# A hybrid DeltaNet and attention layer on one core: sixteen TensorE instructions placed behind named projection matmuls

## Chip, cores and metric

The kernel runs on one core of one Trainium2 chip. The metric is the device time of the whole program in microseconds (us). The kernel before takes 1417.83 us, the median of three runs (1417.33 to 1420.5).

## What is computed

One decoder layer over 1024 tokens of width 1024, all in fp32. Cut to what matters here:

```
u   = rms_norm(h) @ W_in                # one projection, columns shared out to both groups
oA  = gated delta rule                  # 4 heads of 128: conv, decay, chunks of 64, a state
        value, k_cumdecay = solve(eye + lower, rhs)      # unit lower triangular
        step: v_new = value_i - kcd_i @ state
              o     = q_i @ state + intra_i @ v_new
              state = state * exp(gl_i) + k_i^T @ v_new
oB  = diff attention                    # 4 heads, two causal softmax maps of 64 per head
        a = softmax(q1 k1) - lam * softmax(q2 k2);  out = a @ v
h   = h + concat(oA, oB) @ W_out
h   = h + W_down(silu(g) * v),  [g, v] = causal_dwconv3(rms_norm(h) @ W_up)
```

## The kernel before

Tokens are worked on in eight tiles of 128 (`NT`). A number in fp32 is split into a high and a low part, and a product is three TensorE matmuls: high times high, low times high, high times low. So a projection is a long row of matmuls that depend on nothing but loaded weights and the normalised input. Two kinds fill the first half of the program: `gT` (128x512, lines L434 to L436, a head's columns with the tokens along the row) and `pn` (128x256, L415, L416 and L418, tokens along the partitions). In the second half `pwo` (128x512, L395 to L397) multiplies by W_out, and `pe` (L1248 to L1250, in `up_early`) is the first of the products of the up projection.

Stages by time in the profiled execution: first norm up to 45 us; first projections to 95 us; the delta rule of four heads to 385 us; differential attention of four heads from 395 to 675 us; W_out, the second norm and its transposes (`tr`, L257, in `wout_b`) to 745 us; then `up` in 22 blocks and `down` to the end.

The latency-bound parts of a stage are chains through several engines, and projection matmuls lie between their steps on TensorE. In the delta rule, `delta_prep` transposes keys and values (`pk` L625, `pv` L671), `delta_inverse` solves the triangular systems (`pz` L744, L759 and others, each step through VectorE), `delta_scan` steps through the chunks (`pP` L772, `pzz` L776, `pS`, `po` L793; ScalarE evacuates `s` at L781 and the outputs at L794), and `delta_out` scales the output by the gate `szh` (loaded L807, ScalarE L808, GpSimd L809, VectorE L813) and transposes it (`omT` L819). In attention, `qk_norm` and `qk_stack` scale, rotate and stack queries and keys (VectorE L861 to L877, L887, GpSimd L864, ScalarE L886 and L888) and transpose them (`pT` L896, copied out by ScalarE as `K` and `Q` at L897); `attn1` makes a tile of scores (`S` L921, L922, a mask L924), its row maxima (VectorE L926 or L928) and its exponentials `p` (ScalarE L931); `attn2` transposes `p` (`paT` L949) and multiplies by the values (`pao` L954). PSUM gives the scores in attention two tiles, so a third tile of scores can start only when the exponentials of the first are made. `wout_b` adds `pwo` to the residual row (VectorE L1141), scales it (`u` L287) and transposes it (`tr` L257).

Nobody writes the order of the queues by hand: a scheduler takes the instructions one by one by priority (the table `PRI`, applied by `part(name)`) and by its own estimate of when their inputs are there, and puts each on its engine's queue. Each engine works through its queue in order: an instruction that waits holds all that stands behind it on that engine. What of the filler stands ahead of a waiting instruction is therefore fixed when the program is built. All matmuls and transposes go to TensorE directly (`PE = nc.tensor`); `psG`, `psS` and `sm` hand out the PSUM tiles of the stages up to the second norm, `bank` those after it.

Of the kernel before, what the change touches and what calls it, by code (L numbers as in the profile page):

```python
# [10 lines left out]
F32 = mybir.dt.float32  # L11
# [7 lines left out]
P = 128  # L19
# [22 lines left out]
PP0, PP1 = 4, 2  # L42
PRE_K = {5: 1, 6: 0}

A_AT = [(1, 0), (1, 2), (1, 4), (1, 5), (2, 4), (2, 6), (3, 0), (3, 2), (3, 3)]


# [17 lines left out]
def hybrid_layer(ctx, tc, x, positions, norm1_w, w_in, dn_conv_w, dn_a_log, dn_dt_bias,  # L65
                 dn_norm_w, df_q_norm_w, df_k_norm_w, df_lambda_q1, df_lambda_k1,
                 df_lambda_q2, df_lambda_k2, df_subln_w, w_out, norm2_w, w_up, ffn_conv_w,
                 ffn_conv_b, w_down, cst, out, dbg=None, stop=None):
    nc = tc.nc
    V, S, G, PE = nc.vector, nc.scalar, nc.gpsimd, nc.tensor  # L70
    DMA = nc.sync
    dbg = dbg or {}

# [11 lines left out]
    pq = pctx.enter_context(tc.tile_pool(name="pq", bufs=2, space=bass.MemoryType.PSUM))  # L85

    sctx = ExitStack()
    pS = [sctx.enter_context(tc.tile_pool(name="pS", bufs=2, space=bass.MemoryType.PSUM)), 512]
    @contextmanager
    def part(name):  # L90
        p = tc.cur_priority
        q = max(0, p - PRI[name])
        tc.cur_priority = q
        yield
        tc.cur_priority = p + tc.cur_priority - q
# [3 lines left out]
    def nm(s):  # L99
        uid[0] += 1  # L100
        return f"{s}_{uid[0]}"

    def gt(s, shape=(P, T), dt=F32):
        return gp.tile(list(shape), dt, tag="g", name=nm(s))

    def gtr(s):
        return gt(s, dt=F32R)
# [4 lines left out]
    def ct_(s, dt=F32):  # L112
        return cq.tile([P, T], dt, tag="c", name=nm(s))

    def lt(s):
        return lp.tile([P, T], F32, tag="l", name=nm(s))
# [8 lines left out]
        return wp.tile([P, T], F32R, tag="w", name=nm(s))  # L125

    def psG(s="pG"):
        return pq.tile([P, 512], F32, tag="G", name=nm(s), bufs=2)

    def psS(s="pS"):  # L130
        return pS[0].tile([P, pS[1]], F32, tag="S", name=nm(s), bufs=2048 // pS[1])

    def sm(s="sm"):
        return pq.tile([P, 512], F32, tag="t", name=nm(s), bufs=2)

    def small(s, w, bufs=2, dt=F32):
        return sp.tile([P, w], dt, tag=s, name=nm(s), bufs=bufs)
# [69 lines left out]
    def split_w(raw, lo_eng=None, w=T, alloc=None):  # L207
        hi, lo = ((alloc or wt)(s)[:, 0:w] for s in ("whi", "wlo"))
        S.activation(hi, raw[:, 0:w], AF.Copy)  # L209
        if lo_eng is DMA:  # L210

            S.activation(lo, raw[:, 0:w], AF.Copy, scale=-1.0)
            G.dma_start(lo.bitcast(F32), raw[:, 0:w], accum_op=ALU.add)
        elif lo_eng is G:
            G.tensor_tensor(lo, raw[:, 0:w], hi.bitcast(F32), op=ALU.subtract)  # L215
        else:
            V.tensor_tensor(lo, raw[:, 0:w], hi.bitcast(F32), op=ALU.subtract)  # L217
        return hi, lo
# [84 lines left out]
    for k0 in range(0, NK, 3):  # L303
        n = min(3, NK - k0)
# [10 lines left out]
    with tc.manual_schedule(engines={mybir.EngineType.Activation}):  # L315
        for tt in range(NT + 1):
# [7 lines left out]
            if 0 < tt < 4:  # L324
                k = tt - 1
                n = min(3, NK - 3 * k)
# [67 lines left out]
    def mm3(ps, lh, ll, rh, rl, first, last):  # L394
        PE.matmul(ps, lh, rh, start=first, stop=False)  # L395
        PE.matmul(ps, lh, rl, start=False, stop=False)  # L396
        PE.matmul(ps, ll, rh, start=False, stop=last)  # L397
# [43 lines left out]
    def proj_T(h, kind):  # L441
        ct = kind * 4 + h
        st = praw[ct] = ct_("pT")
        for q, o in gemm_T(win, ct * P, xn, lambda q: psG("gT"), DMA):
            S.activation(st[:, q * 512:(q + 1) * 512], o, AF.Copy)
            yield

    def steps(gen, n=99):
        for _ in range(n):
            if next(gen, gen) is gen:  # L450
                break
# [589 lines left out]
    def mix_mm(hl, wf):  # L1041
        ps = psG("pwo")
        for k in range(4):
            wh, wl = wf(k)
            mm3(ps, hl[:, k * P:(k + 1) * P], hl[:, 512 + k * P:512 + (k + 1) * P], wh, wl, k == 0, k == 3)
        return ps
# [104 lines left out]
    def attention():  # L1151
# [27 lines left out]
        for h in range(4):  # L1179
            pr = prep(h + 1) if h < 3 else None  # L1180
            for n, tt in enumerate(range(NT) if h < 3 else reversed(range(NT))):
# [5 lines left out]
                if pr is not None and (PP1 <= n < PP1 + 4 if h > 0 else n >= PP0):  # L1187
                    with part("prep"):
                        steps(pr, 1)
                if (h, n) in A_AT:  # L1190
                    with part("wa"):
# [24 lines left out]
    if stop == "norm2":  # L1216
# [3 lines left out]
    pf = [ctx.enter_context(tc.tile_pool(name=f"pf{i}", bufs=4, space=bass.MemoryType.PSUM, reuse_waits="tile"))  # L1220
          for i in range(2)]

    def bank(i, s):
        return pf[i % 2].tile([P, 512], F32, tag="b", name=nm(s))


    act_dram = dp.tile([FFN, T], F32, name="act_dram")
# [28 lines left out]
    def raw_(s="raw"):  # L1256
        return rp.tile([P, T], F32, tag="raw", name=nm(s))
# [79 lines left out]
    def down():  # L1337
        pairs = [(i, i + 1) for i in range(0, NF, 2)]
        kept = None
        for c in range(2):  # L1340
            cs = slice(c * 512, (c + 1) * 512)
            pss = [bank(tt // 4, "pd") for tt in range(NT)]
            order = pairs if c == 0 else pairs[::-1]
            for pr in order:
                raw = raw_()
                nc.sync.dma_start(raw.rearrange("p (k c) -> p k c", c=512),
                                  wdn[pr[0] * P:(pr[0] + 2) * P, cs].rearrange("(k p) c -> p k c", p=P))
                wh, wl = (t.rearrange("p (k c) -> p k c", c=512) for t in split_w(raw))
                if kept is not None:
                    hl, kept = kept, None  # L1350
                else:
                    hl = []
                    for i in pr:
                        g_ = raw_("act") if c == 0 and pr is order[0] else ct_("act")
                        nc.sync.dma_start(g_, act_dram[i * P:(i + 1) * P, :])
                        gh, gl = gtr("gh"), gtr("gl")
                        S.activation(gh, g_, AF.Copy)  # L1357
                        V.tensor_tensor(gl, g_, gh.bitcast(F32), op=ALU.subtract)  # L1358
                        hl.append((gh, gl))

                def mm(tt, i):
                    ts_ = slice(tt * P, tt * P + P)
                    gh, gl = hl[i]
                    mm3(pss[tt], gh[:, ts_], gl[:, ts_], wh[:, i], wl[:, i],
                        pr is order[0] and i == 0, pr is order[-1] and i == 1)


                tis = [(tt, i) for i in range(2) for tt in range(NT)]
                for tt, i in sorted(tis) if pr is order[-1] else tis:
                    mm(tt, i)  # L1370
            if c == 0:
                kept = hl
            for q in range(4):
                res = lt("fres") if q < 2 else gt("fres")
                rv = res.rearrange("p (t c) -> p t c", c=512)
                rows = slice(q * 256, (q + 1) * 256)
                nc.sync.dma_start(rv, h_dram[rows, cs].rearrange("(t p) c -> p t c", p=P))
                for i in range(2):
                    tt = q * 2 + i
                    V.tensor_tensor(rv[:, i, :], pss[tt], rv[:, i, :], op=ALU.add)  # L1380
                    nc.sync.dma_start(out2[tt * P:(tt + 1) * P, cs], rv[:, i, :])
# [6 lines left out]
    for j in range(NF):  # L1388
        up(j, early[j] if j < EARLY else None)
    down()  # L1390


# [26 lines left out]
```

## Time and profile before

| | |
|---|---|
| median of three runs | 1417.83 us (1417.33 to 1420.5) |
| the profiled execution, its own time | 1418.1 us |
| its span (first to last instruction) | 1416.3 us |
| TensorE (PE) busy | 1337.9 us, 94% |
| VectorE (DVE) busy | 830.9 us, 59% |
| ScalarE (ACT) busy | 634.8 us, 45% |
| GpSimd (POOL) busy | 335.7 us, 24% |
| mean granted TensorE clock | 0.980 of full |

Busy shares are averages over stages that differ. A row of the timeline shows an instruction's start, its duration, its engine and line, what it writes and reads, and in brackets how long its engine stood idle just before it and what ended that. PE is TensorE's matmuls, PEld its weight loads.

### The profile page before, as it was taken

How to read it: one execution, taken by the hardware profiler on the slowest of the kernel's cores; microseconds unless marked ns; L12 is line 12 of the kernel's file. 1: busy time of each engine (PE TensorE's matmuls, PEld its weight loads, DVE VectorE, ACT ScalarE, POOL GpSimd, SP SyncE). 2: the span in 40 equal slices, each digit the busy share in tenths (PEclk: the TensorE clock that was granted, in tenths of full speed). 3: DMA queues.
4: the chain of work that ended last, by engine and by line, in shares of the span. 5: the costliest groups of instructions: out<-in, count | busy, mean ns of one | idle time of the engine just before them, and what ended most of it. 6: DMA issues, size and time to landing. Idle time of an engine off the chain costs nothing. (4 is left out here: it accounts for less than half of the span.)

```text
span 1416.3 us, 21566 instructions
## 1 busy us (share of the span) xinstructions
PE 1337.9 (94%) x8439; PEld 1127.0 (80%) x8439; DVE 830.9 (59%) x1630; ACT 634.8 (45%) x1142; POOL 335.7 (24%) x271
## 2 busy tenths in 40 slices
PE   7999999989979998999878899999999989999998
PEld 7877777878979986778656788888888878888887
DVE  6427767854443368877787666666666666334331
ACT  6467565532234455664544444444444444222220
POOL 3021101120341254240032434444333430000000
PEclk8999999999989999999988999999999999999999
DMA  7353233221733358444421222222222247557421
GB/s 228 89 122 80 64 84 75 76 76 60 210 98 94 106 142 217 113 132 149 142 90 43 80 86 76 89 82 82 89 75 85 79 140 268 172 157 229 137 86 60
DMA packets 145269, 161.54 MB, mean 114 GB/s; under 512 B 9487, under 2 KB 114703, under 8 KB 145167
## 3 DMA queue, kind: packets, MB, share of 16 engines
q1 hardware_dynamic: 130959, 144.21, 32.0%
q0 software_dynamic: 12736, 14.68, 5.6%
q8 instruction: 66, 1.08, 0.3%
q10 hardware_dynamic: 1472, 1.27, 0.3%
q14 instruction: 36, 0.29, 0.1%
HBM read 111.36 MB, written 38.29 MB: 106 GB/s over the span
## 5 line engine op out<-in xcount | busy, mean ns | idle before, releaser
L395 PE MATMUL pd<-whi,gh 128*128 128x512 f32 x352 | 136.9, 389 | 0.0
L396 PE MATMUL pd<-wlo,gh 128*128 128x512 f32 x352 | 136.9, 389 | 0.0
L397 PE MATMUL pd<-whi,gl 128*128 128x512 f32 x352 | 136.9, 389 | 0.0
L415 PE MATMUL pn<-whi,xn 128*128 128x256 f32 x448 | 115.8, 292 | 0.2 <-ACT whi L209 0.2
L416 PE MATMUL pn<-whi,xn 128*128 128x256 f32 x448 | 114.7, 290 | 0.0
L1334 POOL TENSOR_TENSOR acc<-acc,acc 128x1024 f32<-128x1024 f32 x22 | 53.6, 2437 | 242.1 <-issue 215.5
L1357 ACT ACTIVATE gh<-act 128x1024 fp32r<-128x1024 f32 x42 | 44.4, 1060 | 123.9 <-PE pd L396 104.3
L1358 DVE TENSOR_TENSOR gl<-act,gh 128x1024 fp32r<-128x1024 f32 x42 | 52.0, 1241 | 68.0 <-ACT gh L1357 67.7
L415 PEld LDWEIGHTS pn<-whi,xn 128*128 128x128 f32 x448 | 86.9, 195 | 0.7 <-ACT whi L209 0.4
L416 PEld LDWEIGHTS pn<-whi,xn 128*128 128x128 f32 x448 | 86.6, 194 | 0.3
L209 ACT ACTIVATE whi<-raw 128x1024 fp32r<-128x1024 f32 x58 | 61.0, 1053 | 53.1 <-PE pn L416 19.3
L215 POOL TENSOR_TENSOR wlo<-raw,whi 128x1024 fp32r<-128x1024 f32 x22 | 53.2, 2432 | 115.1 <-issue 46.2
L209 ACT ACTIVATE whi<-rx 128x1024 fp32r<-128x1024 f32 x22 | 23.3, 1061 | 127.1 <-POOL rx L1289 127.1
L1248 PE MATMUL pa<-xT,whi 128*128 128x512 f32 x176 | 70.0, 398 | 9.3 <-ACT xT L1121 5.3
L434 PE MATMUL gT<-xn,whi 128*128 128x512 f32 x192 | 77.9, 406 | 0.0
L435 PE MATMUL gT<-xn,whi 128*128 128x512 f32 x192 | 77.6, 404 | 0.0
L436 PE MATMUL gT<-xn,wlo 128*128 128x512 f32 x192 | 77.2, 402 | 0.2 <-DMA wlo<-raw 0.2
L217 DVE TENSOR_TENSOR wlo<-rx,whi 128x1024 fp32r<-128x1024 f32 x22 | 28.9, 1315 | 82.2 <-ACT whi L209 82.1
L395 PEld LDWEIGHTS pd<-whi,gh 128*128 128x128 f32 x352 | 66.1, 188 | 13.8
L396 PEld LDWEIGHTS pd<-wlo,gh 128*128 128x128 f32 x352 | 66.1, 188 | 13.8
L397 PEld LDWEIGHTS pd<-whi,gl 128*128 128x128 f32 x352 | 66.1, 188 | 13.5
L418 PE MATMUL pn<-wlo,xn 128*128 128x256 f32 x448 | 72.4, 296 | 1.5 <-POOL wlo L215 1.5
(380 smaller groups left out, 3691.7 us busy)
## 6 DMA issues: line engine op xcount, KB each, us to landing
act<-act_dram SPq DMA_DIRECT2D x42, 512.0 KB, 4.6
rw<-in_w_up_dram SPq DMA_DIRECT2D x22, 512.0 KB, 3.8
act_dram<-acc SPq DMA_DIRECT2D x22, 512.0 KB, 2.6
raw<-in_w_down_dram SPq DMA_DIRECT2D x22, 512.0 KB, 4.4
raw<-in_w_in_dram SPq DMA_DIRECT2D x18, 512.0 KB, 3.9
pn_dram<-pn SPq DMA_DIRECT2D x16, 512.0 KB, 3.4
wlo<-raw POOLq DMA_DIRECT2D x12, 512.0 KB, 4.6
rx<-in_w_up_dram SPq DMA_DIRECT2D x22, 256.0 KB, 3.0
```

The lines of the kernel that those rows point to most:

```text
L209: S.activation(hi, raw[:, 0:w], AF.Copy)
L395: PE.matmul(ps, lh, rh, start=first, stop=False)
L396: PE.matmul(ps, lh, rl, start=False, stop=False)
L397: PE.matmul(ps, ll, rh, start=False, stop=last)
L415: PE.matmul(o, xs(xn, 0, kt, a, b), wh, start=kt == 0, stop=False)
L416: PE.matmul(o, xs(xn, 1, kt, a, b), wh, start=False, stop=False)
L418: PE.matmul(o, xs(xn, 0, kt, a, b), wf(kt)[1], start=False, stop=kt == NK - 1)
L434: PE.matmul(o, whi[:, kt, :], xs(x_, 0, kt, *qs), start=kt == 0, stop=False)
L435: PE.matmul(o, whi[:, kt, :], xs(x_, 1, kt, *qs), start=False, stop=False)
L436: PE.matmul(o, wlo[:, kt, :], xs(x_, 0, kt, *qs), start=False, stop=kt == NK - 1)
L1248: PE.matmul(ps, wh[:, ks], xh[k], start=first, stop=False, skip_group_check=not start)
L1334: G.tensor_tensor(accs[1], accs[0], accs[1], op=ALU.mult)
```

## The change

A table `BEHIND` names sixteen TensorE instructions, each by a kind of PSUM tile, which tile of that kind, and which instruction into it; and for each another instruction behind which it must stand on the queue. To count them, `PE` becomes a small class that hands each matmul or transpose on to `nc.tensor` and notes it under the tile that it writes. At the end `order_banks()` gives the scheduler sixteen extra order edges without a semaphore. Nothing is computed otherwise, and each engine issues the same instructions as before: 7396 on PE, 1604 on DVE, 972 on ACT.

```diff
+BEHIND = [
+    ("pk", 0, 0, "gT", 9, 12), ("pv", 0, 0, "gT", 11, 3), ("pz", 0, 0, "gT", 14, 22), ("pz2", 1, 0, "gT", 21, 1),
+    ("pzz", 16, 0, "pn", 10, 25), ("omT", 4, 0, "pn", 13, 30), ("S", 0, 1, "pn", 23, 11), ("S", 1, 1, "pn", 23, 11), ("pT", 4, 0, "pn", 24, 47),
+    ("S", 17, 0, "pwo", 3, 11), ("pT", 20, 0, "pwo", 7, 2), ("S", 30, 0, "pwo", 9, 11), ("tr", 18, 0, "pwo", 24, 4),
+    ("tr", 20, 0, "pwo", 26, 9), ("tr", 22, 0, "pwo", 28, 9), ("tr", 29, 0, "pe", 0, 23),
+]
...
-    V, S, G, PE = nc.vector, nc.scalar, nc.gpsimd, nc.tensor
+    V, S, G = nc.vector, nc.scalar, nc.gpsimd
+    banks, by_bank = {}, {}
+    class PE:
+        @staticmethod
+        def note(out, ins):
+            by_bank.setdefault(out.tensor.name.rsplit("_", 1)[0], []).append(ins.ins)
+        @staticmethod
+        def matmul(out, *a, **k):
+            PE.note(out, nc.tensor.matmul(out, *a, **k))
...
+    def bank_name(s):
+        banks.setdefault(s, []).append(nm(s))
+        return banks[s][-1]
+    def order_banks():
+        at = lambda s, n, k: by_bank[banks[s][n]][k]
+        for *x, s, n, k in BEHIND:
+            tc.add_manual_dep(at(*x), at(s, n, k).name,
+                              mybir.DependencyInfo(mybir.DependencyClass.NoSync, mybir.DependencyReason.DATA),
+                              reason="order")
...
-        return pq.tile([P, 512], F32, tag="t", name=nm(s), bufs=2)
+        return pq.tile([P, 512], F32, tag="t", name=bank_name(s), bufs=2)
...
     for j in range(NF):
         up(j, early[j] if j < EARLY else None)
     down()
+    order_banks()
```

(The same edit of the name stands in `psG`, `psS` and `bank`.) The changed file is longer at its head, so a line of the kernel before has a number 36 higher in the change, and all matmuls there carry line L90, all transposes L94, those of the class `PE`.

Since the scheduler takes the other engines' instructions by when their inputs come, their queues change too. Three places follow.

The first is the end of the scan of the third head, on PE. `omT_509` are the transposes of that head's gated output, `pn_593` and `pn_594` two tiles of the next head's projection, `pv1_517` a step of the fourth head's triangular solve. Before:

```order
L415 MATMUL pn_593_3946<-whi_590_3941,xn_14_138 128x256
L732 MATMUL pv1_517_3679<-inv1_511_3504,U_438_3277 32x32 x16
L416 MATMUL pn_593_3946<-whi_590_3941,xn_15_139 128x256
L418 MATMUL pn_593_3946<-wlo_588_3935,xn_14_138 128x256
L819 MATMUL omT_509_3488<-k_sb_96,acc_292_2245 128x128
L418 MATMUL pn_593_3946<-wlo_588_3935,xn_14_138 128x256
```

Now:

```order
L90 MATMUL pn_594_3996<-whi_587_3934,xn_14_138 128x256
L90 MATMUL pn_594_3996<-whi_587_3934,xn_15_139 128x256
L90 MATMUL pn_594_3996<-whi_587_3934,xn_14_138 128x256
L94 MATMUL omT_509_3488<-k_sb_96,acc_292_2245 128x128 x4
L94 MATMUL omT_510_3495<-k_sb_96,acc_292_2245 128x128 x4
L90 MATMUL pv1_517_3679<-inv1_511_3504,U_438_3277 32x32 x16
```

Seven matmuls of `pn_593` and 31 of `pn_594` have come to stand ahead of the transposes, and the sixteen of `pv1_517` behind them.

The second is the same place on ACT, where `s128` and `acc<-po` are the two steps of the scan's last chunks (L781 and L794 before), `szh_508` and `szh_583` the gates of the third and fourth head, and `pn_418` the projection whose columns they are loaded from. Before:

```order
L421 ACTIVATE pn_418_3086<-pn_420_3137 128x512
L209 ACTIVATE whi_599_4151<-raw_598_4149 128x1024
L781 ACTIVATE s128_503_3454<-pzz_502_3452,cj_304_2308 128x128
L794 ACTIVATE acc_292_2245<-po_504_3456,sqs_306_2313 128x128
L713 ACTIVATE inv1_511_3504<-pv0_513_3537 128x256
L800 ACTIVATE dec_271_2044<-acc_292_2245 128x1024
L713 ACTIVATE inv1_511_3504<-pv0_515_3607 128x256
L808 ACTIVATE szh_508_3476<-szh_508_3476 128x1024
L736 ACTIVATE U_438_3277<-inv1_511_3504 32x8x32 x4
L808 ACTIVATE szh_583_3899<-szh_583_3899 128x1024
```

Now:

```order
L457 ACTIVATE pn_418_3086<-pn_420_3137 128x512
L245 ACTIVATE whi_599_4151<-raw_598_4149 128x1024
L817 ACTIVATE s128_479_3400<-pzz_478_3398,cj_304_2308 128x128
...
L830 ACTIVATE acc_292_2245<-po_499_3444,sqs_306_2313 128x128
L844 ACTIVATE szh_508_3476<-szh_508_3476 128x1024
L817 ACTIVATE s128_503_3454<-pzz_502_3452,cj_304_2308 128x128
L844 ACTIVATE szh_583_3899<-szh_583_3899 128x1024
L830 ACTIVATE acc_292_2245<-po_504_3456,sqs_306_2313 128x128
```

The two gates now stand ahead of the last two steps of the scan, and the copy of `pn_418` three chunks earlier than it did.

The third is the start of attention, on PE. `pT_635` to `pT_638` are the transposes of the first head's second half of keys and queries, `S_664` its third tile of scores (`S_643` and `S_657` are the first two), `pn_673` and `pn_684` projections of the values. Before:

```order
L415 MATMUL pn_673_4777<-whi_670_4772,xn_14_138 128x256
L416 MATMUL pn_673_4777<-whi_670_4772,xn_15_139 128x256
L896 MATMUL pT_635_4465<-k_sb_96,stk_634_4460 128x128 x4
L896 MATMUL pT_636_4473<-k_sb_96,stk_634_4460 128x128 x4
...
L418 MATMUL pn_673_4777<-wlo_671_4773,xn_14_138 128x256
L896 MATMUL pT_637_4481<-k_sb_96,stq_633_4459 128x128 x4
L896 MATMUL pT_638_4487<-k_sb_96,stq_633_4459 128x128 x4
L921 MATMUL S_664_4698<-K_610_4365,Q_614_4369 128x384
```

Now:

```order
L90 MATMUL pn_673_4777<-whi_667_4765,xn_15_139 128x256
L90 MATMUL S_664_4698<-K_610_4365,Q_614_4369 128x384
L90 MATMUL S_664_4698<-K_612_4367,Q_614_4369 128x384
...
L90 MATMUL S_683_4841<-K_610_4365,Q_614_4369 128x512
...
L90 MATMUL pn_673_4777<-wlo_671_4773,xn_14_138 128x256 x4
L94 MATMUL pT_635_4465<-k_sb_96,stk_634_4460 128x128 x4
L94 MATMUL pT_636_4473<-k_sb_96,stk_634_4460 128x128 x4
L90 MATMUL pn_684_4854<-whi_667_4765,xn_14_138 128x256
```

`S_664` and the fourth tile `S_683`, which stood behind the transposes, now stand ahead of them and ahead of 36 matmuls of `pn_673`. On DVE, at the same place, the multiplication L861 of the queries and keys, which stood behind the row maxima of `S_643` and `S_657`, now stands ahead of them.

## Rows read from the trace of the kernel before

**Rows 1.** The page's first part: busy time of TensorE over the span.

```profile
PE 1337.9 (94%) x8439; PEld 1127.0 (80%) x8439; DVE 830.9 (59%) x1630; ACT 634.8 (45%) x1142; POOL 335.7 (24%) x271
```

**Rows 2.** Windows: length; PE, PEld, DVE, ACT, POOL busy; granted clock; DMA share, GB/s.

```profile
312.00:330.00 18.00, 13.13 (x156) 11.47 (x157) 9.68 (x18) 5.34 (x9) 5.42 (x4) 0.81 0.25 86
400.00:426.00 26.00, 18.64 (x122) 17.81 (x121) 12.35 (x23) 7.59 (x16) 10.63 (x9) 0.80 0.40 92
534.00:544.00 10.00, 7.64 (x35) 6.22 (x36) 9.56 (x21) 6.70 (x16) 3.89 (x5) 0.83 0.86 235
726.00:738.00 12.00, 7.69 (x25) 5.92 (x25) 9.01 (x17) 9.00 (x15) 4.60 (x4) 0.72 0.35 110
440.00:480.00 40.00, 39.86 (x321) 38.67 (x320) 15.15 (x30) 15.42 (x30) 13.54 (x7) 1.00 0.25 73
850.00:900.00 50.00, 50.00 (x221) 41.13 (x220) 30.69 (x33) 20.79 (x23) 21.79 (x15) 1.00 0.26 84
```

**Rows 3.** Timeline of PE, the delta rule: three of five waiting instructions.

```profile
104.72 0.77 PE L625 MATMUL pk<-k_sb,acc 128*128 128x128 f32 x5 [1.67 <-ACT acc L589]
121.40 0.77 PE L671 MATMUL pv<-k_sb,acc 128*128 128x128 f32 x5 [0.95 <-ACT acc L589]
...
282.74 0.49 PE L776 MATMUL pzz<-nv,U 128*128 128x128 f32 x2 [0.92 <-DVE U L761]
```

**Rows 4.** Timeline of PE, the third head's output transposes.

```profile
317.18 0.33 PE L819 MATMUL omT<-k_sb,acc 128*128 128x128 f32 x1 [2.88 <-DVE acc L813]
320.06 0.47 PE L819 MATMUL omT<-k_sb,acc 128*128 128x128 f32 x1 [1.98 <-DVE acc L813]
```

**Rows 5.** Timeline of ACT around the end of that scan.

```profile
295.60 0.37 ACT L781 ACTIVATE s<-pzz,cj 128x128 f32<-128x128 f32 x1 [1.60 <-DVE s L780]
...
302.47 0.59 ACT L421 ACTIVATE pn<-pn 128x512 f32<-128x512 f32 x1
303.89 0.37 ACT L781 ACTIVATE s<-pzz,cj 128x128 f32<-128x128 f32 x1
313.17 1.06 ACT L808 ACTIVATE szh<-szh 128x1024 f32<-128x1024 f32 x1 [3.35 <-DMA szh<-pn_dram]
```

**Rows 6.** Timeline of PE, the start of attention.

```profile
403.61 0.30 PE L922 MATMUL S<-K,Q 128*128 128x128 f32 x1 [2.82 <-DMA K<-K]
419.62 1.11 PE L896 MATMUL pT<-k_sb,stk 128*128 128x128 f32 x4 [4.54 <-DVE stk L887]
```

**Rows 7.** Timeline of DVE, same stretch.

```profile
406.33 0.42 DVE L928 TENSOR_REDUCE nmx<-S 128x2 f32<-128x256 f32 x1 [3.92 <-PE S L924]
```

**Rows 8.** Timeline of ACT, same stretch.

```profile
418.21 0.63 ACT L886 ACTIVATE stk<-qk 128x512 fp32r<-128x512 f32 x1 [4.43 <-DVE qk L877]
...
421.03 1.19 ACT L897 ACTIVATE K<-pT 128x512 fp32r<-128x512 f32 x2
422.12 0.36 ACT L931 ACTIVATE p<-S,nmx 128x128 f32<-128x128 f32 x1
```

**Rows 9.** Timeline of PE, attention of the second and third head.

```profile
536.36 0.50 PE L921 MATMUL S<-K,Q 128*128 128x512 f32 x1 [3.97 <-ACT p L931]
558.59 0.87 PE L896 MATMUL pT<-k_sb,stk 128*128 128x128 f32 x6 [2.36 <-DVE stk L887]
590.00 0.50 PE L921 MATMUL S<-K,Q 128*128 128x512 f32 x1 [1.32 <-ACT p L931]
```

**Rows 10.** Timeline of PE, transposes of the second norm.

```profile
685.46 0.73 PE L257 MATMUL tr<-k_sb,u 128*128 128x128 f32 x5 [0.95 <-DVE u L287]
...
705.45 0.98 PE L257 MATMUL tr<-k_sb,u 128*128 128x128 f32 x7 [2.30 <-DVE u L287]
730.44 0.87 PE L257 MATMUL tr<-k_sb,u 128*128 128x128 f32 x3 [4.31 <-DVE x L1119]
743.64 1.08 PE L257 MATMUL tr<-k_sb,u 128*128 128x128 f32 x4 [4.57 <-DVE u L287]
```

**Rows 11.** PE's waits between 95 and 750 us: us, times, longest.

```profile
PE pwo L395 <- ACT mhl L1072: 0.7, 1, 0.7
```

More of the change, by code (lines that the diff above doesn't have):

```diff
@@ L69, in hybrid_layer, with transpose @@
     nc = tc.nc
-    V, S, G, PE = nc.vector, nc.scalar, nc.gpsimd, nc.tensor
+    V, S, G = nc.vector, nc.scalar, nc.gpsimd
[7 more added lines that the diff above has]
+            PE.note(out, nc.tensor.matmul(out, *a, **k))
+        @staticmethod
+        def transpose(out, *a, **k):
+            PE.note(out, nc.tensor.transpose(out, *a, **k))
+    def bank_name(s):
[7 more added lines that the diff above has]
+                              reason="order")
     DMA = nc.sync
@@ L127, in psG @@
     def psG(s="pG"):
-        return pq.tile([P, 512], F32, tag="G", name=nm(s), bufs=2)
+        return pq.tile([P, 512], F32, tag="G", name=bank_name(s), bufs=2)
     def psS(s="pS"):
-        return pS[0].tile([P, pS[1]], F32, tag="S", name=nm(s), bufs=2048 // pS[1])
+        return pS[0].tile([P, pS[1]], F32, tag="S", name=bank_name(s), bufs=2048 // pS[1])
     def sm(s="sm"):
-        return pq.tile([P, 512], F32, tag="t", name=nm(s), bufs=2)
+        return pq.tile([P, 512], F32, tag="t", name=bank_name(s), bufs=2)
     def small(s, w, bufs=2, dt=F32):
@@ L1223, in bank @@
     def bank(i, s):
-        return pf[i % 2].tile([P, 512], F32, tag="b", name=nm(s))
+        return pf[i % 2].tile([P, 512], F32, tag="b", name=bank_name(s))
     act_dram = dp.tile([FFN, T], F32, name="act_dram")
```

## The prediction

> **What bounds the kernel.** I read the page's busy table first: TensorE is busy 1337.9 of 1416.3 us [rows 1], so no order of its queue can take off more than the 78.4 us in which it stands idle, and what runs at half clock. [...] Then the timeline of PE, stall by stall: in each row of [rows 3, 4, 6, 9] the bracket says that PE stood before an instruction whose input another engine made late. From the order I then read how much filler now stands ahead of each.
>
> The sum is made against the profiled execution's own time, 1418.1 us, 0.3 above the median. A measurement of this kernel can tell about 0.2% (2.8 us) from no change.
>
> **What the change does to the sum.** It adds no instruction. It moves filler from behind a waiting instruction to ahead of it. That work is borrowed: it would have run later anyway, and where the two orders meet again (before attention, and at the first block of `up`) nothing is left of it. The time gained is idle time truly filled; it is lost again where the next release comes no earlier than before, since PE then waits there instead. If every release stayed at its old time, the gain at any point could be no more than the filler borrowed up to it. If releases move forward with PE, each stall is a gain of its own. That gives two ends for each place.
>
> *Delta rule, first five* [rows 3]: five stalls from 1.67 to 0.92 us, of which three are shown and two between them are like the last, together 5.7. `pk` and `pv` each have eight `gT` more ahead of them, 8 x 0.226 = 1.8 us. It is the same debt carried on, so with fixed releases both together gain 1.8 and not 2.6, and before the fourth stall, where four `gT` (0.9 us) are left of it, only 0.9. Ends: 1.8 (0.9 kept and 0.9 at `pzz`, with 27 `pn` ahead) and 5.7. I take **3.0**, nearer the low end, because the releasers, ACT and DVE, run chains of their own here.
>
> *Output of the third head* [rows 4]: 2.88 + 1.98 = 4.86 us of stall. 38 `pn` now stand ahead, 38 x 0.124 = 4.7 us. The release comes earlier too: the gate `szh` came in at 313.17 us, 10.7 us after `pn` was copied at 302.47 [rows 5], and that copy now stands ahead of the step of the scan that ran at 295.60, three chunks earlier, at about 294. So both stalls go. A new wait takes part of it: the two gates now stand on ACT ahead of the last steps of the scan (303.89 us before). The landing comes to about 294 + 10.7 = 304.7, then two gates of 1.06 us pass first; behind them wait the scan's last `po` on PE and the `pv0` behind it. I price that at 2.0 us (from 0 to 4.9). The window of 312 to 330 us has a clock of 0.81, so 0.19 x 18 = 3.4 us may be had back; I take half, 1.7. Together **4.6**, ends 0 and 8.3.
>
> *Start of attention* [rows 6]: 2.82 + 4.54 = 7.4 us of stall. Ahead of the first score tile stand 24 `pn` more (3.0 us), ahead of `pT` 36 (4.5 us): both covered. But two score tiles come ahead of `pT`, and they need the exponentials of the first two. PE stood before `pT` at 419.62 - 4.54 = 415.1; it will stand before `S_664` four `pn` (0.5 us) and the filled 2.8 us earlier, at 411.8. The exponential it needs ended at 422.12 + 0.36 = 422.5 [rows 8]. Two things bring that forward. The 1.19 us copy of `K` stood ahead of it on ACT and no longer does. And DVE waited 3.92 us for the first scores [rows 7] with the key and query work queued behind; that work now goes first, so the chain through GpSimd to `stk` comes up to 3.9 us earlier. That makes 417.4, a new stall of 5.6 us in place of 7.4. With some 0.8 us for a weight split that moved behind a copy on ACT, I take **1.0**, and nothing of the clock (0.80 in that window), since a stall of 5.6 remains. Ends: 422.5 - 411.8 = 10.7, a loss of 3.3; and 7.4 plus 0.20 x 26 = 5.2 of clock, 12.6.
>
> *Attention, three stalls* [rows 9]: 3.97 + 2.36 + 1.32 = 7.7 us, with 14, 19 and 21 `pwo` more ahead (3.2, 4.3, 4.7 us; the first has eight `pT` besides). They are covered. But in the window around the first DVE is busy 9.56 of 10 us, and so it is, nearly, around the third [rows 2]: there PE waits for an engine that is full. What is filled there leaves less filler for the score and value products that follow. I take half of the stalls, 3.8, and half of the clock's 0.17 x 10 = 1.7 at the first and as much at the third, 3.4 in all: together **5.5**; ends 0 and 11.1. [...]
>
> *Second norm* [rows 10]: the first three `tr` waited 0.95, 2.30 and 2.30, 5.6 us in all (the second, like the third, is not shown). They get 5, 10 and 10 `pwo` ahead (1.1, 2.3, 2.3 us), covered all but exactly. Those `pwo` wait for their own split; one such wait shows in the trace, 0.7 us [rows 11]. Three of them leave **3.4**; ends 0 and 5.6.
>
> *Last pin* [rows 10]: twelve `pe` (2.7 us) go ahead of the `tr` at 730 us, which waited 4.31. But the next `tr`, at 743.64, waits 4.57 us for `u` from DVE, and DVE's work up to it is the same. PE will only wait longer there: **0**; ends 0 and 4.3 + 0.28 x 12 = 7.7.
>
> Sum: 3.0 + 4.6 + 1.0 + 5.5 + 3.4 + 0 = 17.5 us; 1418.1 - 17.5 = 1400.6, so against the median **1400.3 us**. `up` and `down`, half of the time, are dense (50.00 of 50 us in [rows 2]) and keep their order.
>
> The clock's part rests on windows where it fell behind a stall, at the third attention stall behind one of only 1.32 us [rows 9]. [...]
>
> **Rivals.**
>
> *All sixteen fill.* Releases move with PE and the clock stays up: the high ends, 5.7 + 8.3 + 12.6 + 11.1 + 5.6 + 7.7 = 51.0, 1367 us; with half of the difference to mine, 1383. For it: the filler matches the stalls closely, and most releasers are fed by PE itself. Against it: `S_664` and the full DVE.
>
> *The waits move on.* Only the output of the third head gains, since there the release itself comes earlier; elsewhere PE waits at the next release for what it saved. That gives 1418.1 - 4.6 = 1413.5, and to 1419 if the gate's wait takes that too. For it: the debt is paid back before attention. Against it: in the second norm each tile's chain begins with `pwo`, which now comes earlier.
>
> *Slower: the score tiles ahead of their exponentials.* If the work of DVE and GpSimd ahead of `stk` doesn't come forward, the exponential stays at 422.5, PE waits 10.7 us before `S_664`, and the next tile waits again for the second pair. Each copy that those exponentials delay also holds `pn_684`. That is 3.3 us lost, and some 2 more at the second pair; with the gates' 2.0 us and nothing gained elsewhere it gives 1418.1 + 7.3 = about 1425. It decides from the point where the exponential ends later than 411.8 + 7.4 = 419.2 us on the clock of before. For it: an in-order queue on ACT. Against it: the 3.92 us that DVE stood idle.
>
> That the change does nothing can be left out: the order shows all sixteen moves.
>
> **Chances and range.** Forecast 0.55 (1390 to 1411); all fill 0.18 (1367 to 1390); waits move on 0.14 (1411 to 1419); slower 0.13 (1421 to 1428). Faster by over 0.2%: 0.55 + 0.18 and a third of 0.14, 0.78; within 0.2%: the rest of that, 0.09; slower 0.13. From 1376 to 1420 the range leaves out the slower case and a third of all fill, 0.19 together.
>
> **What would show it.** In the changed profile: `omT` without a stall, `szh` on ACT near 304 and no half clock at 319; a stall of 4 to 7 us before `S_664` and none before `pT`; the stalls before the scores at 536 and 590 at half or less; the three `tr` at under 1 us each; the last `tr` waiting some 3 us longer. I would be wrong if `S_664` waits over 8 us, if the `pao` and `pwo` of attention show new stalls of more than 4 us together, or if `up` begins less than 5 us earlier than before.

## The result: slower by 0.9%, and the profile after

The change takes 1432.37 us (median of four, 1425.9 to 1434.85) against 1418.37 before: a ratio of 1.0087, 95% interval 1.0066 to 1.0107. The prediction was 1400.3, with 1376 to 1420 as its range.

The profiled execution of the change took 1431.05 us, its span 1429.3, with a mean clock of 0.971. From its page, the busy times (against [rows 1]):

```profile
PE 1350.6 (94%) x8439; PEld 1134.1 (79%) x8439; DVE 825.2 (58%) x1630; ACT 633.3 (44%) x1142; POOL 335.8 (23%) x271
```

PE's idle time is 1429.3 - 1350.6 = 78.7 us; before it was 78.4. Sixteen stalls were aimed at, and the idle time is the same to 0.3 us; what grew by 12.7 us is PE's busy time, with the same instructions. So stalls moved, and more of the work ran at half of the full TensorE clock: the granted clock is 0.50 for 82.8 us of this execution, for 56.2 us before. But where the time went must be read by place. From here on I compare the start of one and the same instruction in two traces, at points where their orders agree: after the delta rule (before: 393.7 us), after the start of attention (436.3), before the second norm (683.7), at the last `pwo` (718.9), and in the first block of `up` (774.2). Each number says by how many us a stretch, from one point to the next, took longer than in the profiled execution of before:

| stretch | delta rule | start of attention | later attention | second norm | to `up` | sum |
|---|---|---|---|---|---|---|
| the change | +2.0 | -4.3 | +3.3 | +8.2 | +3.3 | +12.6 |

The prediction had -7.6, -1.0, -5.5, -3.4 and 0 there. In the timeline of PE, the rows that answer to [rows 4, 6, 9, 10] (the first is the scan's last output, a new wait):

```profile
320.37 0.38 PE L90 MATMUL po<-s,dec 128*128 128x128 f32 x1 [1.90 <-ACT s L817]
416.71 0.69 PE L90 MATMUL S<-K,Q 128*128 128x384 f32 x1 [4.19 <-ACT p L967]
535.31 0.33 PE L94 MATMUL pT<-k_sb,stk 128*128 128x128 f32 x1 [2.98 <-DVE stk L923]
557.74 0.33 PE L94 MATMUL pT<-k_sb,stk 128*128 128x128 f32 x1 [1.32 <-DVE stk L923]
573.92 0.33 PE L94 MATMUL paT<-k_sb,p 128*128 128x128 f32 x1 [2.35 <-ACT og L1006]
698.93 0.79 PE L90 MATMUL pwo<-whi,mhl 128*128 128x512 f32 x1 [4.32 <-ACT mhl L1108]
713.81 0.80 PE L90 MATMUL pwo<-whi,mhl 128*128 128x512 f32 x1 [4.67 <-ACT mhl L1108]
740.94 0.80 PE L90 MATMUL pe<-x,whi 128*128 128x512 f32 x1 [4.24 <-ACT early L1310]
754.86 0.47 PE L94 MATMUL tr<-k_sb,u 128*128 128x128 f32 x1 [5.50 <-DVE u L323]
```

`omT` has no wait left, nor has the first `pT`; before `S_664` PE waits 4.19 us, as forecast. The largest news are the two `pwo`: the filler itself waits, 4.3 and 4.7 us, longer than the `tr` that it was to cover (2.30 each, [rows 10]).

Why it waits stands on ACT and DVE. Of the change:

```profile
698.28 0.60 ACT L1108 ACTIVATE mhl<-trm 128x512 fp32r<-128x512 f32 x1 [4.31 <-DVE u L323]
704.45 1.25 ACT L1139 ACTIVATE x<-tr 128x512 fp32r<-128x512 f32 x2 [5.58 <-PE tr L94]
```

```profile
696.82 1.28 DVE L323 SCALAR_TENSOR_TENSOR u<-hrow,rs,w2row 128x1024 f32<-128x1024 f32 x1
698.91 0.69 DVE L1109 TENSOR_TENSOR mhl<-trm,mhl 128x512 fp32r<-128x512 f32 x1 [0.80 <-ACT mhl L1108]
```

The split `mhl`, which the `pwo` read, is made on ACT only when DVE has finished `u` of the tile before. That is the very instruction for which `tr` waits. The split's buffer comes from a pool of four that it shares with the residual rows (`hrow`), and the buffer that it gets is a row that `u` reads. So filler and transposes have the same releaser, and the filler has a step more behind it: the first `pwo` starts when the high part is made, 0.60 us on ACT, and the low part takes DVE 0.69 more. At the second of the two tiles it is the same: `u` ends at 713.00 us, and the split starts at 713.16. In the trace of before the same dependence stands, and cost almost nothing, because the eight transposes ran while the split was made:

```profile
695.63 1.06 PE L257 MATMUL tr<-k_sb,u 128*128 128x128 f32 x8 [2.30 <-DVE u L287]
696.45 0.47 PE L395 MATMUL pwo<-whi,mhl 128*128 128x512 f32 x1
```

```profile
695.66 0.60 ACT L1072 ACTIVATE mhl<-trm 128x512 fp32r<-128x512 f32 x1 [3.88 <-DVE u L287]
```

In the change PE stands idle through the split, then runs ten `pwo`, and only then the transposes. ACT waits 5.58 us for those, and behind them on ACT stands the square sum of the next row (L320), from which the next `u` is made. Two tiles go through this one after another.

The granted clock, in windows of the change (280 to 310 is the scan of the third head):

```profile
280.00:310.00 30.00, 27.12 (x196) 25.84 (x194) 22.43 (x68) 8.98 (x18) 7.41 (x4) 0.83 0.12 36
312.00:330.00 18.00, 16.01 (x353) 14.50 (x353) 8.54 (x30) 6.55 (x13) 4.71 (x2) 1.00 0.31 84
400.00:426.00 26.00, 21.53 (x157) 19.48 (x156) 15.61 (x31) 11.25 (x24) 10.36 (x9) 0.87 0.46 120
680.00:730.00 50.00, 40.30 (x179) 31.39 (x179) 31.76 (x112) 19.62 (x41) 1.30 (x1) 0.86 0.31 107
```

Against [rows 2], what was lost at 312 to 330 and at 400 to 426 is had back in whole or in part; new falls stand at 280 to 310 and in the second norm, behind the two waits of `pwo` (before, 680 to 730 had a clock of 0.99). Over the program the mean clock of 0.971, for 0.980, makes some 13 us more of lost clock.

### The profile page after: what moved, and what is told of

Same layout as the page of the kernel before. It is cut to its first block, busy times and chain, and to the rows that moved or that the text cites. A ratio compares the mean times of both kernels' runs of the same rounds, so it can differ in the third digit from the quotient of the medians.

```text
span 1429.3 us, 21573 instructions
## 1 busy us (share of the span) xinstructions
PE 1350.6 (94%) x8439; PEld 1134.1 (79%) x8439; DVE 825.2 (58%) x1630; ACT 633.3 (44%) x1142; POOL 335.8 (23%) x271
## 5 line engine op out<-in xcount | busy, mean ns | idle before, releaser
L90 PE MATMUL pd<-whi,gh 128*128 128x512 f32 x352 | 136.9, 389 | 0.0
L90 PE MATMUL pd<-wlo,gh 128*128 128x512 f32 x352 | 136.9, 389 | 0.0
L90 PE MATMUL pd<-whi,gl 128*128 128x512 f32 x352 | 136.9, 389 | 0.0
L90 PE MATMUL pn<-whi,xn 128*128 128x256 f32 x896 | 131.3, 290 | 0.0
L90 PE MATMUL gT<-xn,whi 128*128 128x512 f32 x384 | 129.0, 408 | 0.0
L90 PE MATMUL pa<-xT,whi 128*128 128x512 f32 x352 | 112.5, 401 | 8.9 <-ACT xT L1157 5.3
L90 PE MATMUL pe<-x,whi 128*128 128x512 f32 x352 | 112.0, 400 | 6.8 <-ACT early L1310 4.2
L90 PEld LDWEIGHTS pn<-whi,xn 128*128 128x128 f32 x896 | 116.4, 193 | 0.9
L90 PE MATMUL pwo<-whi,mhl 128*128 128x512 f32 x256 | 91.1, 422 | 12.9 <-ACT mhl L1108 12.1
L90 PEld LDWEIGHTS pa<-xT,whi 128*128 128x128 f32 x352 | 67.4, 193 | 25.9 <-ACT xT L1157 5.7
L90 PEld LDWEIGHTS pe<-x,whi 128*128 128x128 f32 x352 | 67.6, 193 | 21.7 <-ACT early L1310 4.7
L90 PEld LDWEIGHTS gT<-xn,whi 128*128 128x128 f32 x384 | 71.1, 191 | 12.6
L90 PE MATMUL gT<-xn,wlo 128*128 128x512 f32 x192 | 78.8, 410 | 0.5 <-DMA wlo<-raw 0.5
L90 PEld LDWEIGHTS pd<-wlo,gh 128*128 128x128 f32 x352 | 66.1, 188 | 13.8
L90 PEld LDWEIGHTS pd<-whi,gl 128*128 128x128 f32 x352 | 66.1, 188 | 13.8
L90 PEld LDWEIGHTS pd<-whi,gh 128*128 128x128 f32 x352 | 66.1, 188 | 13.6
```

The source lines that it names most:

```text
L90: PE.note(out, nc.tensor.matmul(out, *a, **k))
```

## The experiments

Each kernel is the change with some pins left out, but for two that move one buffer. A diff of the table shows the pins that stay. The ratios are to the kernel before, run on the same chips.

### Thirteen pins, and the three of the second norm alone

```diff
-    ("S", 17, 0, "pwo", 3, 11), ("pT", 20, 0, "pwo", 7, 2), ("S", 30, 0, "pwo", 9, 11), ("tr", 18, 0, "pwo", 24, 4),
-    ("tr", 20, 0, "pwo", 26, 9), ("tr", 22, 0, "pwo", 28, 9), ("tr", 29, 0, "pe", 0, 23),
+    ("S", 17, 0, "pwo", 3, 11), ("pT", 20, 0, "pwo", 7, 2), ("S", 30, 0, "pwo", 9, 11), ("tr", 29, 0, "pe", 0, 23),
```

> The three pins that put 5, 10 and 10 pwo ahead of the second norm's transposes are left out, the other thirteen stay. Theory A (that filler waits for the same release as the transposes, so PE idles as long as before, the transposes start later, and each tile's chain through ScalarE and VectorE grows; 12.7 us between 648 and 724 us of the changed trace): about 1432.4 - 12.7 = 1419.7 us, from 1416 to 1422, and no pwo wait over 1.5 us in the second norm. Rival B (the loss is the clock's, spread over the program: the mean clock fell from 0.980 to 0.971, 13 us of lost clock time, with new falls in the delta rule at 131, 206, 288 and 305 us that these thirteen pins make): 1425 us or more, clock at 0.975 or lower.

Measured: 1411.03 us, ratio 0.9947 (0.9926 to 0.9968), clock 0.984. It is faster than before, by more than theory A expected. Rival B falls: the same thirteen pins, in the same order up to the second norm, ran at clocks of 0.980 to 0.986, none at 0.975 or lower.

The other way round, only those three stay:

```diff
-BEHIND = [
...
-]
+BEHIND = [
+    ("tr", 18, 0, "pwo", 24, 4), ("tr", 20, 0, "pwo", 26, 9), ("tr", 22, 0, "pwo", 28, 9),
+]
```

> The kernel before with only the three pins of the second norm's transposes. Theory A: 1418.4 + 12.7 = 1431, from 1427 to 1434, with two pwo waits for mhl of more than 4 us, and the delta rule and attention as before. Rival B: under 1423, since nothing in the delta rule moves.

Measured: 1426.25 us, 1.0051 (1.0031 to 1.0070). Slower by 7.5 us, with the rest of the order as before, and with the same two waits (4.33 and 4.69 us) for `mhl`. So these three pins lose by themselves. But 7.5 is less than the 21 us that lie between thirteen pins and sixteen; that is taken up below.

### The split in a buffer of its own

```diff
-        hl = ct_("mhl", F32R)
+        hl = wt("mhl")
```

> All sixteen pins, but the split mhl of a tile's mixed rows takes a buffer of another pool, so that it no longer waits for the residual row of an earlier tile to be read by u. Theory A, in its precise form (the filler's split stands in the buffer that u frees): the pwo waits of over 4 us for mhl go, the filler really stands ahead of the transposes, and the time falls below that of the kernel without those three pins by up to the 5.6 us of stall that they were to fill: 1410 to 1418. Rival C (the pwo wait not for a buffer but for the work ahead of mhl on ScalarE's queue, the exponentials and copies): the waits stay, 1428 to 1434.

Measured: 1419.97 us, 1.0008 (0.9985 to 1.0030), with single runs from 1412.99 to 1427.10. In its timeline the three `pwo` that follow a tile's split:

```profile
693.00 0.47 PE L90 MATMUL pwo<-whi,mhl 128*128 128x512 f32 x1 [0.85 <-DVE hrow L1177]
702.68 0.50 PE L90 MATMUL pwo<-whi,mhl 128*128 128x512 f32 x1 [1.56 <-DVE rs L241]
713.06 0.50 PE L90 MATMUL pwo<-whi,mhl 128*128 128x512 f32 x1 [1.66 <-ACT mhl L1108]
```

The waits of over 4 us are gone, and some 12 of the 21 us with them, by one word that touches none of the sixteen order edges. That the buffer was the cause of those waits is shown; rival C falls. The time stayed above the expected 1410 to 1418, though, 9 us above that of the thirteen pins: with its waits gone the filler still shows no gain. In its trace most of the distance stands behind the last `pwo`. The pool from which the split now comes is that of the weights' splits, and in the first block of `up` PE waits for one of these:

```profile
752.25 0.79 PE L90 MATMUL pc<-xT,whi 128*128 128x512 f32 x1 [4.34 <-ACT whi L245]
```

That the shared buffer has only gone from one wait to another is argued from this row, not shown. The same edit without any pin loses too:

> The kernel before, no pins, with the same other buffer for mhl. Theory A: the transposes still wait for u, but the split can now be made ahead of u and the scheduler may fill by itself: 1412 to 1418.4. Rival C: as before, within 0.2%, 1415.6 to 1421.2.

Measured: 1422.48 us, 1.0031 (1.0015 to 1.0047), slower, against both theories. Its trace stands level with that of before up to the last `pwo` (+0.2 us) and loses 4.3 us from there to `up`; the kernel with the pins loses 4.7 in the same place. What the other buffer does there without the pins wasn't followed.

### The four places one by one

```diff
-BEHIND = [
...
-]
+BEHIND = [
+    ("pk", 0, 0, "gT", 9, 12), ("pv", 0, 0, "gT", 11, 3), ("pz", 0, 0, "gT", 14, 22), ("pz2", 1, 0, "gT", 21, 1),
+    ("pzz", 16, 0, "pn", 10, 25), ("omT", 4, 0, "pn", 13, 30),
+]
```

> The six pins of the delta rule alone (pk, pv, pz, pz2, pzz, omT). Theory A (each place's gain is what its own stalls lose until the two orders meet again before attention): the trace with thirteen pins stood 3.8 us ahead of before at that meeting point (380.8 for 384.6), so about 1418.7 - 3.8 = 1415, from 1412 to 1419. Rival B (the falls of the clock in the solve, which came in some executions of this same order and not in others, take it all): 1418 to 1423.

Measured: 1418.74 us, 0.9993 (0.9978 to 1.0009), with single runs from 1412.5 to 1421.7. Level with before.

```diff
-BEHIND = [
...
-]
+BEHIND = [
+    ("S", 0, 1, "pn", 23, 11), ("S", 1, 1, "pn", 23, 11), ("pT", 4, 0, "pn", 24, 47),
+]
```

> The three pins at the start of attention alone (two score tiles, pT). Theory A: 4.2 us gained between 386 and 430 us in both traces that have them (the stalls of 2.8 and 4.5 us become one of 4.2 to 4.6, and 10.2 us at half clock become 6.8), about 1414.5, from 1412 to 1417. The prediction's own price for this place was 1.0. Rival: what is gained is lost at the next DVE-bound stretch (scores at 536 us), 1418 within 2.

Measured: 1415.78 us, 0.9986 (0.9978 to 0.9995). A gain of 2.8 us by the medians; one wait of 4.60 us before `S_664` in place of two.

```diff
-BEHIND = [
...
-]
+BEHIND = [
+    ("S", 17, 0, "pwo", 3, 11), ("pT", 20, 0, "pwo", 7, 2), ("S", 30, 0, "pwo", 9, 11),
+]
```

> The three pins in attention of the later heads alone. Theory A (there the waits only move: pT 3.0, paT 2.3 to 2.8 in place of the scores 4.0 and 1.3): within 0.2% of before, 1416 to 1421. The prediction's price was a gain of 5.5, so 1413; a loss of a few us would say that the moved waits cost more than those they replace.

Measured: 1425.21 us, 1.0053 (1.0041 to 1.0065): slower by 6.6 us, against theory A too. Its stretch of later attention is 4.6 us longer than before. The `pT` waits are those of the change, but there is a new wait on ACT that nothing of before resembles:

```profile
578.15 0.37 ACT L1005 ACTIVATE og<-pao,sums 128x128 f32<-128x128 f32 x1 [2.97 <-DMA mix_dram<-og]
```

An output tile waits until the store of the head before has left its buffer. On SP the store stands behind another transfer:

```profile
571.07 0.33 SPq L1094 DMA_DIRECT2D xa<-in_x_dram  x1
572.37 0.37 SPq L1015 DMA_DIRECT2D mix_dram<-og  x1
```

The load of `xa` was issued 1.3 us before the store; in the trace of before it was issued at 560.08, nearly 9 us before the store (568.91). The store took 5.7 us to land here, and 2.3 in the trace of before. It is so in all fourteen traces: in the four with these three pins the load goes out 0.9 to 1.5 us before the store, the store lands after 5.4 to 6.2 us, and ACT waits 2.7 to 3.4 us for its buffer; in the ten without them the load is 8.8 to 10.5 us ahead, the store lands after 2.3, and ACT doesn't wait. The pins let `pwo` run early, which frees the buffer for this load at another time. That the load is what delayed the store is argued from the traces; a kernel that holds it back wasn't tried.

```diff
-BEHIND = [
...
-]
+BEHIND = [
+    ("tr", 29, 0, "pe", 0, 23),
+]
```

> The last pin alone (twelve pe ahead of the transposes at 730 us). Theory A (the next transposes wait for the same VectorE work; PE waits as long in other places): 1417 to 1421, with the 4.3 us stall gone and one of 4 to 5 us before pe or the next transposes. Rival: the order before lost real time there, a gain of 2.7 or more, under 1416.

Measured: 1415.28 us, 0.9971 (0.9959 to 0.9984). A gain of 3.3 us where the prediction had 0, and theory A had none either; the rival's number holds. The twelve `pe` are not what gains: PE now waits before them, longer than it did before `tr` (4.31 us in [rows 10]):

```profile
732.43 0.63 PE L87 MATMUL pe<-x,whi 128*128 128x512 f32 x1 [5.02 <-ACT early L1307]
```

With this pin the scheduler also moved an instruction on DVE: the scaling `u` of the last row now stands ahead of the split `wlo` of a weight's part `ry`, where before (and in the change) it stands behind. (The table has three lines less here than in the change, so L320 and L91 here are L323 and L94 there.) Before, and with the last pin alone:

```profile
739.80 1.22 DVE L217 TENSOR_TENSOR wlo<-ry,whi 128x1024 fp32r<-128x1024 f32 x1
741.12 2.37 DVE L287 SCALAR_TENSOR_TENSOR u<-hrow,rs,w2row 128x1024 f32<-128x1024 f32 x1
```

```profile
739.17 1.94 DVE L320 SCALAR_TENSOR_TENSOR u<-hrow,rs,w2row 128x1024 f32<-128x1024 f32 x1
742.24 1.21 DVE L250 TENSOR_TENSOR wlo<-ry,whi 128x1024 fp32r<-128x1024 f32 x1
```

And its timeline, for the last `tr`, which waited 4.57 us in [rows 10]:

```profile
741.26 0.30 PE L91 MATMUL tr<-k_sb,u 128*128 128x128 f32 x1 [1.03 <-DVE u L320]
```

That this place on DVE makes the gain is argued from the traces: in the four with the last pin and none in the second norm, `u` stands ahead and the stretch is 3.1 to 3.8 us shorter than before. No kernel moves this one instruction alone.

### Together

```diff
-BEHIND = [
...
-]
+BEHIND = [
+    ("pk", 0, 0, "gT", 9, 12), ("pv", 0, 0, "gT", 11, 3), ("pz", 0, 0, "gT", 14, 22), ("pz2", 1, 0, "gT", 21, 1),
+    ("pzz", 16, 0, "pn", 10, 25), ("omT", 4, 0, "pn", 13, 30), ("S", 0, 1, "pn", 23, 11), ("S", 1, 1, "pn", 23, 11),
+    ("pT", 4, 0, "pn", 24, 47), ("tr", 29, 0, "pe", 0, 23),
+]
```

> The pins of the delta rule, of the start of attention and the last one, ten in all; the three of later attention and the three of the second norm are left out. Theory A (each place stands for itself: delta 0.0, start 2.8 and last 3.3 us gained when alone; later attention lost 6.6, the second norm 7.5): by the single runs 1418.6 - 6.1 = 1412.5; counted back from the thirteen pins (1411.0), with later attention's loss of 4 to 7 taken out, 1404 to 1407. So 1404 to 1413. Rival (the places eat each other's gain, a pin's gain is the next one's filler): 1415 to 1419.

Measured: 1411.39 us, 0.9943 (0.9921 to 0.9964), single runs from 1404.97 to 1413.41: in theory A's range, and under the rival's.

```diff
-BEHIND = [
...
-]
+BEHIND = [
+    ("S", 0, 1, "pn", 23, 11), ("S", 1, 1, "pn", 23, 11), ("pT", 4, 0, "pn", 24, 47), ("tr", 29, 0, "pe", 0, 23),
+]
```

> The pins of the start of attention and the last one alone, four in all. Theory A: 1418.6 - 2.8 - 3.3 = 1412.5, from 1410 to 1414. If the delta rule's pins do gain when the clock stays up, this stands above the ten pins; if they don't, level with them.

Measured: 1411.10 us, 0.9949 (0.9934 to 0.9965). Level with the ten. So the delta rule's six pins are worth nothing that can be told, and the version to keep is the four pins: faster than before by 0.5%, and than the change by 21 us.

But the thirteen are level with both (1411.03), though they hold the three pins of later attention, which alone lose 6.6 us. In the traces that loss is there with thirteen pins too (+4.2 us, for -1.2 with ten). The medians hide it, since the executions of the thirteen had more of the clock: four of their six ran at 0.984 to 0.986 (1409.5 to 1411.7 us), and two of the ten's six (1405.0 and 1405.8); the others, at 0.980 and 0.981, took 1414.2 to 1414.5 and 1410.9 to 1413.4. Whether the pins have a part in that difference of the clock stays open.

```diff
-BEHIND = [
...
-]
+BEHIND = [
+    ("tr", 18, 0, "pwo", 24, 4), ("tr", 20, 0, "pwo", 26, 9), ("tr", 22, 0, "pwo", 28, 9), ("tr", 29, 0, "pe", 0, 23),
+]
```

> The three pins of the second norm's transposes with the last one. If places add: 1418.6 + 7.5 - 3.3 = 1422.8. Theory D (the last pin's gain turns into a loss behind the other three: in the changed trace that stretch lost 3.3 us where alone it gained 3.8): 1428 or more, which would account for most of the distance between thirteen pins and sixteen (21 us) and the 7.5 of the three alone.

Measured: 1430.16 us, 1.0085 (1.0065 to 1.0105). By addition it would be 1422.8; theory D holds. With the three pins of the second norm beside it, the last pin leaves `u` of the last row behind the weight's split, and the last `tr` waits 5.50 us in place of 1.03, in this trace as in that of the change. These four pins alone give nearly the whole loss of the change (1.0087).

So of the 21 us between thirteen pins and sixteen, 15 are the three pins in the last one's company: 11.9 lost here, 3.3 gained by the last alone. The rest stands in the traces in the delta rule (+2.0 for -3.8), where both have the same order on every engine; it is taken up at the end.

```diff
-BEHIND = [
...
-]
+BEHIND = [
+    ("omT", 4, 0, "pn", 13, 30),
+]
```

> The one pin of the third head's output transposes. The prediction's term was a gain of 4.6 (ends 0 and 8.3), so 1414. Theory A (the two stalls of 4.9 us go, and a wait for the gate behind the scan comes, 1.3 to 1.9 in the traces that have this pin): 1414 to 1416. Rival (the gates' wait and the lost filler behind it take all): 1417 to 1420.

Measured: 1425.70 us, 1.0063 (1.0045 to 1.0081). Slower by 7.5 us, where the prediction's term was a gain of 4.6 and both theories had at most no loss. Its timeline:

```profile
323.93 0.26 PE L87 MATMUL pz<-inv 32*32 32x32 f32 x2 [5.38 <-DVE inv L772]
366.83 0.47 PE L91 MATMUL omT<-k_sb,acc 128*128 128x128 f32 x1 [4.98 <-DVE acc L846]
```

The two stalls of [rows 4] are gone, and two longer ones have come: one in the fourth head's triangular solve, 6 us later, and one at the same transposes of the fourth head, which had no such wait before. The delta rule is 10.3 us longer in this trace, part of it by the clock, which was granted at half for 13.7 us from 323 and for 6.8 from 364. Beside the other five pins of the delta rule this one costs nothing (1418.74 for all six); why is not shown.

The stretches of the twelve traces, read as in the table above:

| kernel | delta rule | start of attention | later attention | second norm | to `up` |
|---|---|---|---|---|---|
| 13 pins | -3.8 | -4.3 | +4.2 | +1.0 | -3.1 |
| norm pins | +2.0 | -2.2 | -1.0 | +9.4 | -0.6 |
| 16 pins, split free | -1.4 | -3.6 | +3.7 | -0.7 | +4.7 |
| no pins, split free | +2.0 | -0.4 | +0.1 | -1.5 | +4.3 |
| delta rule's pins | +2.4 | -1.1 | -0.8 | 0.0 | +0.1 |
| attention's start | +2.0 | -3.6 | -0.3 | +0.1 | -0.1 |
| later attention | +1.9 | -0.7 | +4.6 | -0.6 | -0.4 |
| last pin | +1.3 | -0.5 | +0.4 | +0.1 | -3.8 |
| ten pins | -3.3 | -4.8 | -1.2 | 0.0 | -3.7 |
| four pins | +1.1 | -3.7 | -2.2 | +1.5 | -3.3 |
| norm and last | +0.8 | -0.5 | -0.1 | +9.5 | +2.8 |
| output pin | +10.3 | -2.2 | -0.4 | +0.1 | -0.4 |

Where a stretch has the order of before it should read 0. The delta rule reads +0.8 to +2.0 there, the start of attention -0.4 to -2.2, later attention -2.2 to +0.4: so far single executions differ, and the profiled one of before was quick in the first and slow in the second.

## Why the prediction was wrong

**Second norm: the step that failed.** "Those `pwo` wait for their own split; one such wait shows in the trace, 0.7 us [rows 11]. Three of them leave 3.4." The price was taken from PE's row, where the wait was short because the transposes ran during the split. What the split itself waits for stands in ACT's row of before, `mhl` after 3.88 us for `u`, and I didn't read it. It is the releaser of the stall that was to be covered. In place of a gain of 3.4 the three pins alone lose 7.5 us; up to the last `pwo` their trace has 5.1 us more in gaps, and 10.2 us at half clock where before has none. The sign "the three `tr` at under 1 us each" came true all the same: it watched the transposes, and the wait had gone to the filler.

**Last pin.** "DVE's work up to it is the same": it isn't. The order of DVE changes with the pin, in two ways: alone it gains 3.3 us, behind the norm pins it loses. The sum took the places for independent, and here they aren't: 7.5 and -3.3 make 11.9, not 4.2.

**Later attention.** A gain of 5.5 was forecast; the pins lose 6.6. The first half of the argument held (DVE paces, the waits move to `pT` and `paT`); the window that it gives for the third stall is not among [rows 2]. It reads:

```profile
588.00:598.00 10.00, 7.89 (x35) 6.07 (x35) 9.31 (x22) 7.53 (x16) 3.94 (x7) 0.83 0.69 165
```

What was left out is SP's queue: a load that was issued at another time, and a store that took 3.4 us longer to land; that this is the whole of the loss is not shown.

**Delta rule and output.** 3.0 + 4.6 were forecast, and the six pins alone lose 0.1. In their trace PE's gaps in the delta rule shrank by 1.4 us only, from 23.5 to 22.1, of the 10.6 aimed at, and the half clock grew from 17.1 to 23.9 us. Of the output the signs came as forecast: no wait at `omT`, a wait for the gate ahead of the scan's end (`po` 1.90 us for a price of 2.0), no half clock at 319. But the reason that was given, "The release comes earlier too", failed. The order on ACT is the one that was read, but the scan itself comes later with the filler ahead of it: its first `pzz` starts at 293.85 us for 282.74, `pn` is copied at 308.70 where I had about 294, and `szh` is made at 319.00 (after a wait of 2.08) where I had 304 and before had 313.17. What releases `omT` comes 10.5 us later than before, not earlier:

```profile
316.68 4.64 DVE L813 SCALAR_TENSOR_TENSOR acc<-acc,ro,szh 128x128 f32<-128x128 f32 x8 [3.75 <-POOL szh L809]
```

```profile
327.20 2.19 DVE L849 SCALAR_TENSOR_TENSOR acc<-acc,ro,szh 128x128 f32<-128x128 f32 x8
```

`omT` has no wait because it too comes later, at 328.88 for 317.18. And "both stalls go" counted the filler as if it cost nothing to take it: by itself the pin takes it from the fourth head, which then waits 4.98. That debt was in the prediction as a bound, 0; the measured value, a loss of 7.5, lies beyond it.

**The clock.** The prediction had 3.4 us of it back; some 13 us more were lost. In the window of 400 to 426 us the clock rose only from 0.80 to 0.87, with a wait of 4.2 us left in it, and new falls came where the waits went: 0.83 at 280 to 310 us (1.00 before), with PE idle for 2.9 us of it in place of 0.9, and 0.86 at 680 to 730 (0.99 before). That a filled stall gives its clock back was my estimate; the trace doesn't test it, for the stalls weren't filled, only moved.

**Start of attention: right.** The wait before `S_664` was forecast at 5.6 us and is 4.2 to 4.6, `pT` waits no more, and these pins alone gain 2.8 us for the 1.0 forecast. The end of the exponential came early enough, so the slower rival did not decide: the change is slower, but not by its mechanism.

**The sum.** Measured by themselves the terms are 0.1 us lost in the delta rule with the output, 2.8 gained, 6.6 lost, and 11.9 lost in the second norm with the last pin: a loss of 15.8 in place of a gain of 17.5. The change measured a loss of 14.0. So two terms had the wrong sign, the second norm and later attention; one, the delta rule with the output, gave nothing; and the last pin's changed its sign in company. The prediction had named its own sign of this: `up` was to begin at least 5 us earlier, and it began 12.6 us later. The filler's prices are [rows 2] by the matmul, 0.124 us for each of the 321 `pn` and 0.226 us for each of the 221 of 512 columns; in the same trace, at a granted clock of 1.00, `gT`, `pwo` and `pe` start 0.23 us apart too.

**The rivals.** That the waits move on had 0.14 and stopped at 1419; it is the nearest to what happened, and its missing half is that a moved wait can be longer than the one that it replaces.

## What to carry to other kernels

Before putting filler ahead of a waiting instruction, read what the filler waits for, on the engine that makes its input and down to the buffer which that input takes: with the same releaser as the wait it only adds its own steps. Filler is borrowed from the next place, and an order edge on one engine changes the queues of the others, a load here, a weight's split there. So test such edges place by place and in pairs; here four of the sixteen gave as much as ten or thirteen.

## What the runs showed of the hardware

The same order of instructions ran the delta rule at different clocks. In the window of 280 to 310 us, ten pins and the delta rule's pins alone, whose orders agree there:

```profile
280.00:310.00 30.00, 27.12 (x227) 25.55 (x226) 22.69 (x71) 10.44 (x23) 6.12 (x4) 1.00 0.24 72
```

```profile
280.00:310.00 30.00, 27.11 (x196) 25.98 (x196) 22.64 (x69) 8.54 (x18) 7.42 (x4) 0.83 0.11 36
```

PE is busy 27.1 of 30 us in both, but with 227 matmuls in one and 196 in the other: the granted clock is 1.00 in one and 0.83 in the other. (The two stand some us apart by then, so the windows don't hold quite the same instructions.) In the change it was 0.83 too, and its delta rule ended 5.8 us later than that of the thirteen pins, with the same order on every engine, and with 27.3 us at half clock there for 13.7. So the order alone doesn't fix the clock of this stretch. Single runs of these two kernels spread by 8.4 and 9.2 us (standard deviation 3.5 and 3.4); those of the kernel before, in samples of 11 to 26, by 7.2 to 9.8 (1.8 to 2.3). What tips the clock was not found.
